# Attention's gating on VectorE in two steps, and the sample tile's LayerNorm on VectorE

## The chip, the cores and the metric

The kernel runs on one core of a Trainium2 chip. Its time is the device time of one execution in microseconds (us); the figure that counts is the median of several executions. Six units work side by side and meet at semaphores: TensorE (PE, with PEld for its weight loads), VectorE (DVE), ScalarE (ACT), GpSimd (POOL), SyncE (SP, which here only issues transfers) and the DMA engines. Each engine takes its own instructions strictly in their order. SP, ACT and POOL each issue transfers from that same order, so an issue that has to wait also holds what stands behind it.

## The reference

A two-layer decoder step for a prompt of 2048 rows and 8 samples of 8 rows (64 rows), model width 1024. Layer 0 ("even") has a pooling mixer and a differential attention with 4 heads; layer 1 ("odd") is a gated linear attention. What the change touches is the end of the attention's head and the layer's LayerNorm:

```python
o = diff_attn_prompt(qf, kf, vf, lam_full)        # softmax(q1 k1) - lambda softmax(q2 k2), times v
o = (rms_norm(o, subln_w) * (1.0 - lam_init)).reshape(b, t, DA_WIDTH).astype(x.dtype)
mix = jnp.concatenate([pool_out * jax.nn.silu(pg), o * jax.nn.silu(ag)], axis=-1)
y = layer_norm(DN_ALPHA * x + mix @ w_out, ln_g, ln_b)
```

So each row of a head's output (128 values) is scaled by one over its root mean square and multiplied by a gate, silu(ag), value by value. The LayerNorm then works on rows of 1024.

## The kernel before

The even layer runs in four stretches. First the input projection, to about 540 us, with head 0's first work woven in. Then head 0 of the attention beside out_pool, the pooling half of the output projection (to about 740). Then head 1 beside Sample, the samples' own attention over cached keys and values (to about 890). Then heads 2 and 3 beside out_attention, which is the attention half of the output projection and the LayerNorm (to about 1236). The odd layer fills the rest.

`weave` (L861) interleaves a main generator (Attention.units, L1109) with a fill generator by declared costs. The program so built is then put in order by a scheduler that simulates it, with the scores of the attention given priority. So a change of which engine does a step changes the order on every engine, wherever the simulated times move.

In `Attention`, the 16 tiles t of 128 query rows are taken one after the other, each for the heads of the stretch. `load_q` (L971) loads 256 rows of queries by two transfers on SP's queue into qr (two buffers), which `split` (L37) cuts into a high part qh on ScalarE and a low part ql on GpSimd; `load_gate` (L985) loads the gate of the same 256 rows, sga (four buffers), on SP's queue. `scores` (L992) makes the scores sc on PE (L1016, L1017), their row maximum nm on VectorE and the exponentials e on ScalarE (L1036). `pv` (L1056) transposes e on PE (tp, L1068), copies the result on ScalarE (aT) and multiplies it by the values (po, L1061). It then copies po to oq (L1088) and sums its squares on VectorE (sqq, L1090). After each second tile, `rms_scale` (L2309) makes the row scale rmo from both tiles' sums: small VectorE steps L2320, L2322, a power on GpSimd (L2333) and VectorE L2325. Then come the gating steps that are changed, on oq of 128 x 2 x 128. For heads 0 and 1 a GpSimd transfer writes oq to memory; heads 2 and 3 leave it in place for out_attention. There are 16 tiles and 4 heads, so 32 such pairs.

In `out_attention`, `tile_` (L1221) transposes one row tile of the mixed heads on PE (otp, L1227: two from om, loaded from memory, and two from oq of heads 2 and 3), splits it into oh and ol, multiplies it by the output weights (op, L51 to L53) and calls LayerNorm's `finish` (L1284). The row tiles come in the order 0 to 13, 16, 14, 15, where tile 16 is the 64 sample rows. `turn` (L1237) transposes the finished rows for the odd layer. `finish` has two ways to apply root, mean, gain and bias to z: four VectorE steps in two halves with one transfer each on SP's and ScalarE's queues (urgent, L1293 to L1301), or three GpSimd steps over all 1024 values and a GpSimd transfer (L1302 to L1305).

`Sample` (L2098) loads its inputs on SP's queue: the page table, the samples' queries and new keys (sqr, skn), the new values (svn), constants, and then for every page the cached keys (sk) and values (sv), to addresses that SP reads from the page table. Its first products on PE are ssc (L2170), from sk.

## Time and profile before

| | before |
|---|---|
| median of 3 runs | 2129.9 us (2129.59 to 2132.04) |
| profiled execution | 2135.73 us |
| its span, first to last instruction | 2133.9 us |
| mean granted TensorE clock | 0.975 of full speed |
| TENSOR_SCALAR L1097 (gating, GpSimd) | 64 instructions, median 367 ns |
| TENSOR_TENSOR L1099 (gating, GpSimd) | 32 instructions, median 734 ns |

The profile is that of one execution. A row of the timeline gives the start, the duration, the engine, the line, the operation and its tiles (out<-in), the count of instructions that the row groups, and in square brackets how long the engine stood idle before it and what released it. In a row of waits stand who waited for whom, the sum, the number of waits and the longest. A row of a group gives its sum and the mean of one in ns; a row with three numbers divided by strokes gives minimum, median and maximum in ns. Rows of queues end in "q": SPq is SyncE's own list of transfers, and the duration there is that of the issue. The groups quoted with 14 or 64 instructions are those between 560 and 1232 us.

### The profile page before, as it was taken

What the parts mean: (1) busy time and instruction counts of PE and PEld (TensorE: products, weight loads), DVE (VectorE), ACT (ScalarE), POOL (GpSimd) and SP (SyncE); (2) the same over time, 40 slices, a digit from 0 to 9 for tenths busy, and PEclk for the clock granted to TensorE, in tenths of its full rate; (3) what the DMA queues carried; (4) which work ended last, traced back from release to release, by engine and by line L of the source; (5) the groups of instructions that cost most, each with busy time, mean ns of one, the idle gap of its engine ahead of it and who ended that gap; (6) DMA issues with size and microseconds to landing.
All of it is one profiled execution on the core that took longest, in us unless ns stands there. A gap on an engine that the chain in (4) does not pass through costs nothing. (4 is left out here: it accounts for less than half of the span.)

```text
span 2133.9 us, 31445 instructions
## 1 busy us (share of the span) xinstructions
PE 2005.8 (94%) x10769; PEld 1641.6 (77%) x10769; DVE 1486.8 (70%) x2762; ACT 1005.2 (47%) x1910; POOL 878.9 (41%) x1163
## 2 busy tenths in 40 slices
PE   8999998999999999888898899999999997999998
PEld 7878786877788777677777678788888776888786
DVE  7697657565876676798767667756733647888884
ACT  4244433345633465665555443445425655555552
POOL 2345444323754542567643504222211223466554
PEclk9999999999899999999999999999999998999998
DMA  8877777547864588563322458765643557556532
GB/s 288 278 241 238 256 260 233 168 110 198 276 203 152 169 294 284 157 202 121 119 72 65 146 187 281 253 205 199 198 146 121 180 163 242 165 170 204 164 130 109
DMA packets 210973, 407.75 MB, mean 191 GB/s; under 512 B 29186, under 2 KB 106370, under 8 KB 210802
## 3 DMA queue, kind: packets, MB, share of 16 engines
q1 hardware_dynamic: 140354, 234.57, 36.1%
q0 software_dynamic: 49664, 156.39, 20.8%
q10 hardware_dynamic: 20784, 14.68, 2.2%
q8 instruction: 87, 1.43, 0.3%
q14 instruction: 84, 0.69, 0.1%
HBM read 277.99 MB, written 127.55 MB: 190 GB/s over the span
## 5 line engine op out<-in xcount | busy, mean ns | idle before, releaser
L1036 ACT ACTIVATE e<-sc,nm 128x896 f32<-128x896 f32 (+11 forms) x192 | 164.8, 864 | 125.5 <-DVE nm L1034 87.3
L1021 DVE TENSOR_REDUCE nm<-sc 128x1 f32<-128x768 f32 (+7 forms) x160 | 156.8, 991 | 27.9 <-PE sc L1017 16.3
L45 DVE TENSOR_TENSOR wk<-wr,wk 128x1024 fp32r<-128x1024 f32 x80 | 98.3, 1229 | 101.3 <-ACT wk L40 100.8
L45 DVE TENSOR_TENSOR wl<-wr,wh 128x1024 fp32r<-128x1024 f32 (+1 forms) x90 | 108.7, 1211 | 80.7 <-ACT wh L40 76.8
L1016 PE MATMUL sc<-kst,qh 128*128 128x512 f32 (+9 forms) x352 | 136.5, 391 | 29.3 <-ACT e L1036 28.2
L1061 PE MATMUL po<-vt,aT 128*128 128x128 f32 x1088 | 155.4, 282 | 2.2 <-ACT aT L1073 2.1
L40 ACT ACTIVATE wh<-wr 128x1024 fp32r<-128x1024 f32 (+1 forms) x85 | 88.0, 1038 | 138.7 <-PE f L52 62.4
L1061 PEld LDWEIGHTS po<-vt,aT 128*128 128x128 f32 x1088 | 140.4, 197 | 9.0 <-ACT aT L1073 2.4
L40 ACT ACTIVATE wk<-wr 128x1024 fp32r<-128x1024 f32 x77 | 81.4, 1058 | 134.1 <-PE f L53 96.2
L1073 ACT ACTIVATE aT<-tp 128x512 f32<-128x512 f32 (+3 forms) x160 | 85.4, 534 | 103.0 <-PE tp L1068 102.4
L1017 PE MATMUL sc<-kst,ql 128*128 128x512 f32 (+9 forms) x352 | 123.8, 354 | 0.0
L1016 PEld LDWEIGHTS sc<-kst,qh 128*128 128x128 f32 x352 | 69.3, 197 | 49.9 <-ACT e L1036 40.6
L1068 PE MATMUL tp<-ident,e 128*128 128x128 f32 x544 | 92.4, 285 | 13.1 <-ACT aT L1073 11.8
L1045 DVE SCALAR_TENSOR_TENSOR e<-e,c,e 128x128 f32<-128x128 f32 (+15 forms) x64 | 96.0, 1499 | 1.4
L1068 PEld LDWEIGHTS tp<-ident,e 128*128 128x128 f32 x544 | 64.5, 145 | 28.2 <-ACT aT L1073 16.7
L1017 PEld LDWEIGHTS sc<-kst,ql 128*128 128x128 f32 x352 | 69.7, 198 | 4.1 <-issue 0.2
L1039 DVE TENSOR_TENSOR s<-s 128x1 f32<-128x1 f32 x64 | 21.2, 331 | 70.2 <-ACT e L1036 69.9
L1092 POOL TENSOR_SCALAR s1q<-s 128x1 f32<-128x1 f32 x64 | 16.9, 266 | 104.4 <-DVE s L1039 79.5
L53 PE MATMUL op<-wh,ol 128*128 128x512 f32 x128 | 52.3, 408 | 5.1 <-DVE ol L1232 5.1
L51 PE MATMUL op<-wh,oh 128*128 128x512 f32 x128 | 53.1, 415 | 1.2 <-ACT oh L1231 1.2
L51 PE MATMUL gz<-wh,gmh 128*128 128x512 f32 x128 | 51.5, 406 | 1.8 <-ACT gmh L40 1.8
L53 PE MATMUL gz<-wh,gml 128*128 128x512 f32 x128 | 51.1, 402 | 1.9 <-DVE gml L45 1.9
(882 smaller groups left out, 6658.2 us busy)
## 6 DMA issues: line engine op xcount, KB each, us to landing
wr<-in_w_q SPq DMA_DIRECT2D x75, 512.0 KB, 4.9
wr<-pt SPq DMA_DIRECT2D x40, 512.0 KB, 7.3
wr<-rt SPq DMA_DIRECT2D x40, 512.0 KB, 4.2
sk<-in_cachek SPq DMA_DIRECT2D x64, 256.0 KB, 3.7
sv<-in_cachev SPq DMA_DIRECT2D x64, 256.0 KB, 4.8
pt<-pn POOLq DMA_DIRECT2D x32, 256.0 KB, 7.2
qr<-q SPq DMA_DIRECT2D x64, 128.0 KB, 3.9
kr<-k SPq DMA_DIRECT2D x32, 256.0 KB, 4.4
```

The costliest lines, as they stand in the source:

```text
L40: h = nc.scalar.activation(hi, raw, AF.Copy)
L45: return h, (lo_eng or nc.vector).tensor_tensor(out=lo, in0=raw, in1=hi, op=ALU.subtract)
L51: nc.tensor.matmul(ps, lh(k), rh(k), start=(first and k == 0), stop=False, **kw)
L53: nc.tensor.matmul(ps, ll(k), rh(k), start=False, stop=(last and k == n - 1), **kw)
L1016: nc.tensor.matmul(o, qh[:, c, qs], kst[:, ks], start=True, stop=False)
L1017: nc.tensor.matmul(o, ql[:, c, qs], kst[:, ks], start=False, stop=k < npc - 1)
L1021: nc.vector.tensor_reduce(out=nm[:, c, i:i + 1], in_=p[:, :, :w], op=ALU.max, axis=AX.XY, negate=True)
L1036: nc.scalar.activation(o, p, AF.Exp, bias=nm[:, m, 0:1], accum_out=s[:, m, i if npc > 1 else 0:][:, :1])
L1045: nc.vector.scalar_tensor_tensor(out=es[0][:, :nk], in0=es[1][:, :nk], scalar=c2, in1=es[0][:, :nk], op0=ALU.mult, op1=ALU.add)
L1061: nc.tensor.matmul(po, s[:, 128 * j:128 * j + 128], vt[:, k0 + j, :], start=(k0 + j == 0), stop=(k0 + j == n - 1))
L1068: nc.tensor.transpose(p[:, 128 * j:128 * j + 128], a[:, 128 * (k0 + j):128 * (k0 + j) + 128], self.ident)
L1073: nc.scalar.activation(s[:, :128 * g], p[:, :128 * g], AF.Copy)
```

## The change

Two edits. In `pv`, two GpSimd steps that scale each of the two tiles by its rows' factor, and one GpSimd step that multiplies both by the gate, become two VectorE steps, one per tile, that do both at once. In `tile_`, the list of tiles that take LayerNorm's urgent way is widened from 14 and 15 to all above 13, which adds tile 16.

```diff
@@ Attention.pv
             for i in range(2):
-                nc.gpsimd.tensor_scalar(out=oq[:, i, :], in0=oq[:, i, :], scalar1=sc[:, i:i + 1], scalar2=1.0,
-                                        op0=ALU.mult, op1=ALU.mult)
-            nc.gpsimd.tensor_tensor(out=oq, in0=oq, in1=sg, op=ALU.mult)
+                nc.vector.scalar_tensor_tensor(out=oq[:, i, :], in0=oq[:, i, :], scalar=sc[:, i:i + 1], in1=sg[:, i, :],
+                                               op0=ALU.mult, op1=ALU.mult)
@@ out_attention.tile_
-        ln.finish(d["y0"][t0:t0 + n, :], i in (14, 15))
+        ln.finish(d["y0"][t0:t0 + n, :], i > 13)
```

From line 1098 on, every line of the new program has a number lower by one (L1097 is the new gating step, L1227 becomes L1226, L2325 becomes L2324, and so on). The scheduler's order changes with it; two places show this.

The first is SP's queue early in head 1, at the loads ahead of the sample's cache keys. In the names, qr_5, qr_6 and qr_7 are head 1's query loads for its last three blocks of 256 rows (two transfers each, in two buffers), sga_2 is the gate of its third block, kr are keys, zr and zx belong to out_pool, and pages and sqr to Sample. Before:

```order
L977 DMA qr_5_7714<-q_57 64x2x256 x2
L1171 DMA zx_0_6447<-in_x 64x512
L963 DMA kr_1_9574<-k_58 64x2x512 x2
L1171 DMA zx_1_6448<-in_x 64x512
L977 DMA qr_6_8075<-q_57 64x2x256 x2
L2106 DMA pages<-in_page_table 1x64
L2112 DMA sqr<-q_57 64x4x64
```

And with the change:

```order
L1170 DMA zx_0_6440<-in_x 64x512
L963 DMA kr_1_9557<-k_58 64x2x512 x2
L977 DMA qr_6_8063<-q_57 64x2x256
L1170 DMA zx_1_6441<-in_x 64x512
L977 DMA qr_6_8063<-q_57 64x2x256
L977 DMA qr_7_8447<-q_57 64x2x256 x2
L989 DMA sga_2_7013<-sg_60 128x2x128
L2105 DMA pages<-in_page_table 1x64
L2111 DMA sqr<-q_57 64x4x64
```

Two loads of qr_7 and one of a gate, sga_2, now stand between qr_6 and the page table; before, they stood behind the first cache loads.

The second is VectorE at the end of the attention, where oq_2 and oq_3 are the last tiles of heads 2 and 3 and oz is the sample tile's row block. Before:

```order
L1278 SCALAR_TENSOR_TENSOR oz_12535,lnso_16_12863<-oz_12535,op_1_12875 64x512
L1090 SCALAR_TENSOR_TENSOR sqq_2_12657,ssq_2_12367<-oq_2_12366 128x128
L1288 TENSOR_SCALAR lnso_16_12863<-lnso_16_12863 64x1
L2320 TENSOR_TENSOR rmoa_2_12660<-rmoa_2_12660,ssq_2_12367 128x2
L2322 TENSOR_SCALAR rmoa_2_12660<-rmoa_2_12660 128x2
L2325 TENSOR_TENSOR rmoa_2_12660<-rmoa_2_12660,rmra_2_12661 128x2
L1291 TENSOR_SCALAR lnso_16_12863<-lnso_16_12863 64x1
L1090 SCALAR_TENSOR_TENSOR sqq_3_12719,ssq_3_12459<-oq_3_12458 128x128
```

And with the change:

```order
L1287 TENSOR_SCALAR lnso_16_12831<-lnso_16_12831 64x1
L1290 TENSOR_SCALAR lnso_16_12831<-lnso_16_12831 64x1
L1295 SCALAR_TENSOR_TENSOR oz_12505<-oz_12505,lnso_16_12831,lng 64x512 x2
L1090 SCALAR_TENSOR_TENSOR sqq_2_12627,ssq_2_12337<-oq_2_12336 128x128
L1297 SCALAR_TENSOR_TENSOR oz_12505<-oz_12505,lnso_16_12831,lnb 64x512 x2
L2319 TENSOR_TENSOR rmoa_2_12630<-rmoa_2_12630,ssq_2_12337 128x2
L2321 TENSOR_SCALAR rmoa_2_12630<-rmoa_2_12630 128x2
L2324 TENSOR_TENSOR rmoa_2_12630<-rmoa_2_12630,rmra_2_12631 128x2
L1097 SCALAR_TENSOR_TENSOR oq_2_12336<-oq_2_12336,rmoa_2_12630,sga_7_11730 128x128 x2
L1090 SCALAR_TENSOR_TENSOR sqq_3_12688,ssq_3_12429<-oq_3_12428 128x128
```

The four LayerNorm steps of the sample and the gating of head 2's last tiles now stand on VectorE ahead of sqq_3. On PE, the transposes of oq_2 and oq_3 for row tile 14 (otp) stood one behind the first eight products po of head 3's last tile and one behind all of them:

```order
L1061 MATMUL po_3_12673<-vt_8755,aT_3_4_12686 128x128 x4
L1227 MATMUL otp_12916<-ident,oq_2_12366 128x128
L1068 MATMUL tp_3_12_12703<-ident,e_3_0_12375 128x128 x4
L1061 MATMUL po_3_12673<-vt_8755,aT_3_8_12697 128x128 x4
L1061 MATMUL po_3_12673<-vt_8755,aT_3_12_12708 128x128 x4
L1227 MATMUL otp_12916<-ident,oq_3_12458 128x128
```

And with the change both stand behind them:

```order
L1068 MATMUL tp_3_12_12672<-ident,e_3_0_12345 128x128 x4
L1061 MATMUL po_3_12642<-vt_8741,aT_3_8_12666 128x128 x4
L1061 MATMUL po_3_12642<-vt_8741,aT_3_12_12677 128x128 x4
L1226 MATMUL otp_12886<-ident,oq_2_12336 128x128
L1226 MATMUL otp_12886<-ident,oq_3_12428 128x128
```

Only the place of the first transpose has moved there.

## The prediction

> **What bounds the kernel now.** I read the busy shares first, then the windows by stage, then TensorE's waits in the stages that the diff touches, and last the timeline around the longest of them.
>
> ```profile
> PE 2005.8 (94%) x10769; PEld 1641.6 (77%) x10769; DVE 1486.8 (70%) x2762; ACT 1005.2 (47%) x1910; POOL 878.9 (41%) x1163
> 560.00:740.00 180.00, 176.91 (x1000) 149.67 (x998) 125.32 (x246) 74.74 (x164) 95.71 (x137) 0.98 0.64 194
> 740.00:880.00 140.00, 132.30 (x1419) 99.85 (x1418) 96.32 (x275) 81.19 (x202) 48.04 (x81) 0.99 0.82 260
> 920.00:1200.00 280.00, 251.68 (x1552) 212.71 (x1552) 219.57 (x460) 153.65 (x328) 149.44 (x156) 0.98 0.34 106
> 1200.00:1240.00 40.00, 30.13 (x164) 25.05 (x164) 25.02 (x46) 19.79 (x36) 18.86 (x18) 0.83 0.65 202
> 1240.00:1300.00 60.00, 60.00 (x277) 49.46 (x276) 39.99 (x71) 19.59 (x33) 10.68 (x18) 1.00 0.57 190
> ```
>
> The columns after a window's length are the busy time of PE, PEld, DVE, ACT and POOL, then the granted clock, the DMA share and GB/s. PE is the bound: 94% of the whole. The changed steps run from 560 to 1230 us. In head 0 (560 to 740) PE is idle for 3.1 us, in head 1 (740 to 880) for 7.7, in heads 2 and 3 (920 to 1200) for 28.3 us, with VectorE next at 219.57 of 280 and GpSimd at 149.44. From 1200 to 1240 PE is idle a quarter of the time, at a clock of 0.83; from 1240 on it is busy without a break. So what PE gains or loses up to 1240 stands in the end time, and GpSimd's 41% by itself is worth nothing: what counts is the waits of PE that end on it.
>
> ```profile
> PE sc L1016 <- ACT e L1036: 10.8, 10, 2.9
> PE otp L1227 <- POOL oq L1099: 7.8, 3, 6.1
> ```
>
> These are PE's two largest waits from 920 to 1232. The first is the softmax chain, which the change doesn't touch in itself. The second ends on the very GpSimd step that the change removes, 7.8 us in three waits, of which one is 6.1. That one is the tail of attention:
>
> ```profile
> 1216.04 0.54 POOL L2333 TENSOR_TENSOR lnso<-lnso,rsqeo 64x1 f32<-64x1 f32 x1
> 1218.72 2.01 PE L1061 MATMUL po<-vt,aT 128*128 128x128 f32 x16
> 1220.76 0.28 ACT L1088 ACTIVATE oq<-po 128x128 f32<-128x128 f32 x1 [1.25 <-PE po L1061]
> 1220.95 2.33 POOL L1304 TENSOR_TENSOR oz<-oz,lnb 64x1024 f32<-64x1024 f32 x1
> 1221.07 2.36 DVE L1090 SCALAR_TENSOR_TENSOR sqq<-oq 128x128 f32<-128x128 f32 x1 [5.12 <-ACT oq L1088]
> 1223.92 0.71 POOL L2333 TENSOR_TENSOR rmoa<-rmoa,rsqea 128x2 f32<-128x2 f32 x1 [0.64 <-DVE rmoa L2322]
> 1225.25 0.71 POOL L1097 TENSOR_SCALAR oq<-oq,rmoa 128x128 f32<-128x128 f32 x2
> 1226.83 0.48 PE L1227 MATMUL otp<-ident,oq 128*128 128x128 f32 x1 [6.10 <-POOL oq L1099]
> 1223.40:1233.60 10.20, 6.09 (x14) 4.59 (x15) 4.92 (x13) 5.49 (x10) 2.72 (x5) 0.50 0.74 242
> ```
>
> PE ends its last product at 1220.73 and stands until 1226.83. In between: the copy of oq, its square sum sqq on VectorE, which here lasts 2.36 us beside the sample LayerNorm's L1304, the power on GpSimd, and the three gating steps. After such a stand the clock is halved: 0.50 for the 10.2 us of the last row.
>
> **The change part by part.**
>
> ```profile
> L2250 DVE SCALAR_TENSOR_TENSOR ssq<-so,rmos,ssg x8: 339/341/1353, 900.5 to 903.6; 128x128 f32<-128x128 f32 x8
> L1090 DVE SCALAR_TENSOR_TENSOR sqq<-oq x64: 264/286/2496, 562.3 to 1221.1; 128x128 f32<-128x128 f32 x64
> L1090 DVE SCALAR_TENSOR_TENSOR sqq<-oq 128x128 f32<-128x128 f32 x64 | 33.5, 523 | 9.2 <-ACT oq L1088 8.9
> 1212.54 0.68 DVE L1278 SCALAR_TENSOR_TENSOR oz<-oz,op 64x512 f32<-64x512 f32 x1
> L1303 POOL TENSOR_TENSOR oz<-oz,lng 128x1024 f32<-128x1024 f32 x14 | 34.3, 2447 | 0.8
> L1304 POOL TENSOR_TENSOR oz<-oz,lnb 128x1024 f32<-128x1024 f32 x14 | 35.5, 2538 | 0.5
> L1097 POOL TENSOR_SCALAR oq<-oq,rmoa 128x128 f32<-128x128 f32 x64 | 27.2, 433 | 13.1 <-DVE rsqea L2332 6.1 <-DVE rmoa L2325 2.8 <-DVE c L1043 1.6
> L1099 POOL TENSOR_TENSOR oq<-oq,sga 128x256 f32<-128x256 f32 x32 | 26.9, 844 | 1.3
> ```
>
> The new gating step has the form of L2250 (two SBUF tensors, a scalar per row, 128x128): 0.341 us. VectorE gets 64 x 0.341 = 21.8 us, and 4 x 0.68 = 2.7 us for the sample's LayerNorm. GpSimd loses 27.2 + 26.9 = 54.1 us of gating, and the sample's steps.
>
> **1. The tail, a gain.** Worked forward from these rows. The sample's root is there at 1216.58. VectorE's four new LayerNorm steps and the square sum of the third head, which the order puts among them, take 4 x 0.68 + 0.29 = 3.0, to 1219.6. The third head's scale and gating follow: 0.45 for two small steps, 0.74 with the power, 0.26 for the last factor, 0.68 for two gating steps, to 1221.7. PE doesn't wait for this, since its transpose now stands behind the last products. The fourth head's oq is there at 1221.04, so VectorE is 0.7 late; its square sum ends at 1222.1, the power starts at 1222.55 and ends at 1223.3, the gating ends at 1224.15, and PE starts at 1224.25 in place of 1226.83: **-2.6 us**. The gap falls from 6.1 to 3.5 us. The halved stretch is 10.2 us, of which 6.8 follow the restart and cost 3.4 us of work; I take **-1.0** for it, between 0 and -3.4, because the restart now falls earlier into a stretch that may still begin. From 1240 on no other engine holds PE, so the gain carries.
>
> [...]
>
> **2. Head 1's last query load, a gain.** The order moves two loads of qr_7 on SP's queue from amid the cache loads to ahead of the page table.
>
> ```profile
> 817.41 0.63 ACT L40 ACTIVATE qh<-qr 128x512 fp32r<-128x512 f32 x1 [6.30 <-DMA qr<-q]
> 818.98 0.46 PE L1016 MATMUL sc<-kst,qh 128*128 128x416 f32 x1 [2.55 <-ACT e L1036]
> 820.60:824.00 3.40, 3.40 (x16) 1.47 (x15) 3.36 (x5) 0.89 (x3) 0.56 (x1) 0.51 0.92 301
> ```
>
> ScalarE stood 6.30 us before this split, with the exponentials queued behind it, and PE 2.55 us for those; a window at 0.51 followed and cost 1.7 us of its 3.4. With the load some 80 us earlier both go: **-4.3 us**, at least 0 if another wait takes that place.
>
> **3. The price of that move.** SP takes its loads in order. In the new order qr_7 (two loads) and then sga_2 wait for a buffer, and the page table, the sample's inputs and the cache keys stand behind them.
>
> ```profile
> 714.92 1.23 SPq L977 DMA_DIRECT2D qr<-q  x2
> 716.20 0.49 SPq L2106 DMA_DIRECT2D pages<-in_page_table  x1
> 718.71 0.68 SPq L2112 DMA_DIRECT2D skn<-k  x1
> 725.18 0.47 SPq L2121 DMA_DIRECT2D svn<-v  x1
> 726.96 0.38 SPq L2131 DMA_DIRECT2D smask<-in_s_mask  x1
> 728.46 16.93 SPq L2142 DMA_DIRECT2D sk<-in_cachek  x10
> 729.69 1.26 POOL L45 TENSOR_TENSOR ql<-qr,qh 128x512 fp32r<-128x512 f32 x1
> 729.75 1.23 DVE L2325 TENSOR_TENSOR rmoa<-rmoa,rmra 128x2 f32<-128x2 f32 x1
> 731.88 0.34 SPq L2142 DMA_DIRECT2D sk<-in_cachek  x1
> DMA to landing us min/median/max: 3.0/3.2/3.4
> 742.75 1.06 PE L2170 MATMUL ssc<-sk,sqs 128*32 128x512 f32 x8
> ```
>
> Two query buffers exist, so qr_7 waits for head 1's ql two loads earlier, done at 730.95. sga_2 waits for the gating of head 0's rows right behind L2325, which with two VectorE steps is done at 731.7. Page table, sample inputs and the small constants then take what they took before (716.20 to 719.4 and 725.18 to 727.3: 5.4 us, and a further 1.1 to the first key load at 728.46; the wait between them is for PE and is over by then), so the first key load comes at about 739.2 and the fourth, 731.88 before, at 742.6, landed at 745.8 with 3.2. PE asks at 742.75: a stand of 3.1, in place of a slack of 7.7. Part of a later wait for the softmax is absorbed, part comes back as a halved window of 1.7: **+4.0**, between 0 (if the buffers come free sooner) and +8 (each us beyond that point is one of PE's).
>
> **4. The transpose wait in head 3.**
>
> ```profile
> 1112.84 0.33 PE L1227 MATMUL otp<-ident,oq 128*128 128x128 f32 x1 [1.50 <-POOL oq L1099]
> ```
>
> Its 1.50 us go, but for the new steps' own length: **-1.3**.
>
> **5. VectorE's new work.** Half of the 21.8 us, 10.9, fall where VectorE is busy 219.57 of 280. Below heads 0 and 1 PE is busy at least 94% of its time, and that hides the other half. How much of 10.9 reaches PE no row shows: at least 0, since 60 us of VectorE are idle there and the steps leave GpSimd, which shortens its queue for everyone; at most 10.9 and the holds. L1090 shows the holds: 286 ns by the median, 523 by the mean, 2496 at most, beside GpSimd steps. L1303 and L1304 take 69.8 us of the 280, a quarter; of 16 pairs of new steps 4 would meet one, at half its 2.5 us: 5 us. So 0 to +16; I take **+2.5**, the quarter of 10.9 by which VectorE's idle share is not enough, since a step can only delay PE if the softmax chain is then late. GpSimd's removed steps held VectorE too, which goes the other way and is in the lower end.
>
> [...]
>
> **6.** The order also changes inside the odd layer (the first 60 us and around 1800), without new work: 0, within 3 either way.
>
> Sum: -2.6 - 1.0 - 4.3 + 4.0 - 1.3 + 2.5 = **-2.7 us**. The profiled execution took 2135.73 (span 2133.9 and 1.8 around it), 5.8 over the median of the runs; it would become 2133.0, and the median 2129.9 becomes **2127.2**.
>
> **The rivals.**
> - **More is gained:** the key loads are not late (term 3 is 0: no stand at the first ssc), the halved windows at the tail go (-3.4) and VectorE's idle time takes the new steps (term 5 is 0): -2.7 - 4.0 - 2.4 - 2.5 = -11.6, 2118.3. For it speaks that each wait named is a measured one; against it, that VectorE's idle time in heads 2 and 3 is in pieces around a chain which PE already waits on, 10.8 us.
> - **The queue eats it:** SP stands longer than I think (term 3 at +8): +1.3, 2131.2. It decides when the first keys land past 750.
> - **Slower: VectorE becomes the wait in heads 2 and 3.** The new steps sit ahead of the row maxima that the exponentials need. If all 10.9 us and the holds of 5 land on PE, term 5 is +16: -2.7 + 13.5 = +10.8, 2140.7; with half of that +4, 2133.9. It passes the -2.7 of the rest as soon as over 5.2 of those 16 us reach PE, and shows slower from about 9.5. The softmax wait of 10.8 us with VectorE at 78% speaks for it; that the removed GpSimd steps held VectorE too speaks against it.
> - **It doesn't do what it says:** PE waits for the transposes elsewhere as much as before, with the tail alone at -1: terms 1 and 4 nearly nothing, +1, 2131. Little speaks for it, since the wait's releaser is removed.
>
> **How the numbers follow.** About 0.2%, 4.3 us, can be told from no change: 2125.6 to 2134.2. The forecast has 0.42, with an own range of 2122 to 2132 (a third of it below 2125.6); more is gained 0.24; the queue eats it 0.07; slower 0.23; not as said 0.04. Faster: 0.24 + 0.14 = 0.38. Slower: 0.22, with 0.01 of that rival inside the bound. The same: the rest, 0.40. The range reaches half way into both outer cases, 2116 to 2138.
>
> **What would show it.** Tail: the wait of otp on oq at 3.5 us, released by VectorE L1097, sqq at 0.29, no GpSimd step of 2.3 us beside it. Head 1: no ScalarE wait for qr near 817. SP: qr_7 about 731, the first key load about 739, a PE wait for sk of about 3 us. Heads 2 and 3: VectorE's sum up by some 11 us, PE's wait for e at 10.8 to 14. I am wrong if that wait grows by over 8, if the keys come later than 745, or if new steps of 2 us and more stand in a row.

## The result, and the profile after

| | before | after |
|---|---|---|
| median of 5 runs each | 2129.59 us (2128.41 to 2132.04) | 2153.94 us (2152.93 to 2160.76) |
| ratio of after to before | | 1.0117, 95% interval 1.0104 to 1.013 |
| profiled execution | 2135.73 us | 2160.76 us |
| its span | 2133.9 us | 2159.0 us |
| mean granted TensorE clock | 0.975 | 0.969 |

The changed kernel is slower by 24.4 us, where 2.7 us less had been forecast. One run of a later kernel, that with heads 0 and 1 changed, took 2290.72 us at a granted clock of 0.825 and counts in no median or ratio here. The profiled execution of the changed kernel is 6.8 us over its median, that of before 6.1, so the two profiles can be compared. First the busy shares of the changed kernel, as the page gives them:

```profile
PE 2019.4 (94%) x10769; PEld 1650.6 (76%) x10769; DVE 1501.9 (70%) x2830; ACT 1006.6 (47%) x1910; POOL 811.1 (38%) x1063
```

By these GpSimd lost 68 us of work (878.9 before) and VectorE took 15 (1486.8). TensorE has the same 10769 matmuls, but they last 14 us longer, and its mean granted clock is lower (0.969 against 0.975). So I looked for the stage in which that happens. These are the windows of the changed kernel, with the columns as in the prediction (the third after the colon is PE's busy time, the last three numbers are granted clock, DMA share and GB/s):

```profile
560.00:740.00 180.00, 175.84 (x991) 148.62 (x992) 123.59 (x264) 74.39 (x164) 83.33 (x119) 0.98 0.62 188
740.00:880.00 140.00, 133.57 (x1437) 100.61 (x1435) 101.42 (x287) 82.53 (x207) 37.18 (x61) 1.00 0.85 274
880.00:930.00 50.00, 36.76 (x197) 29.32 (x195) 42.06 (x107) 27.80 (x75) 28.95 (x30) 0.73 0.74 217
930.00:1200.00 270.00, 236.23 (x1425) 200.06 (x1424) 208.09 (x431) 137.91 (x295) 110.41 (x101) 0.95 0.28 86
```

And those windows of the kernel before which the prediction hasn't shown:

```profile
880.00:930.00 50.00, 37.25 (x244) 30.96 (x237) 44.54 (x107) 32.21 (x85) 36.38 (x42) 0.90 0.70 217
930.00:1200.00 270.00, 243.75 (x1496) 205.88 (x1496) 211.01 (x431) 146.66 (x311) 141.84 (x147) 0.98 0.31 97
```

Up to 880 us hardly anything is lost. From 880 to 930 the clock is 0.73 in place of 0.90, and 197 matmuls start in place of 244; from 930 to 1200 it is 0.95 in place of 0.98, and 1425 start in place of 1496. VectorE's share of the second window is no larger (208.09 of 270 us against 211.01), though it is a share of less work.

Windows of equal length hold unequal work, so I cut both traces after equal numbers of matmuls instead, at the start of the 4520th and of the 6640th (the end of head 1 to just behind the attention). These are nearly the same matmuls: ahead of the first cut 16 of the 4520 differ, ahead of the second 2 of the 6640. The same view, first of before, then of after:

```profile
0.00:865.82 865.82, 825.19 (x4520) 664.97 (x4523) 600.11 (x1133) 378.53 (x702) 372.39 (x615) 0.98 0.73 228
865.82:1252.16 386.34, 337.47 (x2130) 282.76 (x2121) 295.40 (x609) 209.50 (x452) 202.57 (x211) 0.96 0.40 125
1252.16:2133.90 881.74, 843.13 (x4131) 693.85 (x4129) 591.33 (x1020) 417.19 (x757) 303.98 (x338) 0.97 0.55 184
```
```profile
0.00:867.30 867.30, 826.19 (x4520) 665.07 (x4521) 604.05 (x1165) 379.42 (x704) 345.81 (x573) 0.99 0.72 228
867.30:1272.64 405.34, 347.48 (x2130) 289.60 (x2121) 311.50 (x646) 209.46 (x449) 164.79 (x152) 0.92 0.38 119
1272.64:2159.00 886.36, 845.75 (x4131) 695.94 (x4129) 586.30 (x1020) 417.76 (x757) 300.48 (x338) 0.97 0.54 183
```

Of the 25.1 us between the spans, 19.0 lie in the middle stretch (405.34 against 386.34), 1.5 ahead of it and 4.6 behind. The 1.3 us by which after is late at the 2000th matmul (489.6 against 488.3), ahead of the first changed step, are in the 1.5. In the middle the matmuls are busy 10.0 us longer (347.48 against 337.47), and PE's idle time, length less busy, goes from 48.9 to 57.9 us. So about half of the loss is more waiting, and half is the clock, which is halved for 65 us of the stretch in place of 34. VectorE works 16.1 us more there (311.50 against 295.40), 77% and 76% of the stretch. PE's waits from 880 to 1262 of after, then of before without its largest wait for oq, which the prediction shows:

```profile
PE sc L1016 <- ACT e L1036: 18.3, 21, 3.0
PE op L53 <- DVE ol L1231: 11.4, 5, 3.7
PE tp L1068 <- ACT aT L1073: 11.2, 16, 1.8
PE po L1061 <- ACT aT L1073: 5.0, 3, 4.0
PE otp L1226 <- DVE oq L1097: 4.2, 2, 2.4
PE tp L1068 <- DVE e L1045: 3.2, 1, 3.2
```
```profile
PE sc L1016 <- ACT e L1036: 18.1, 16, 3.4
PE tp L1068 <- ACT aT L1073: 8.0, 14, 0.8
PE op L53 <- DVE ol L1232: 5.1, 5, 2.1
PE po L1061 <- ACT aT L1073: 2.1, 2, 1.8
```

The wait for the gating fell from 7.8 to 4.2 us, as meant. The wait for the softmax's exponentials is the same. What grew are waits for steps that the change doesn't touch: the low parts ol for out_attention (+6.3), the transposed exponentials aT (+3.2 and +2.9), one wait for e (3.2, new). None of them is large; they are spread over the stretch.

The largest single one stands where head 1 ends. The timeline of after around it:

```profile
894.44 4.50 DVE L2249 SCALAR_TENSOR_TENSOR ssq<-so,rmos,ssg 128x128 f32<-128x128 f32 x3
896.26 5.08 POOL L969 TENSOR_TENSOR kst<-kr,kst 64x512 fp32r<-64x512 f32 x4
898.87 0.94 DVE L1024 TENSOR_REDUCE nm<-sc 128x2 f32<-128x768 f32 x1
899.92 0.58 ACT L1036 ACTIVATE e<-sc,nm 128x384 f32<-128x384 f32 x1 [1.21 <-DVE nm L1024]
901.13 1.67 PE L1061 MATMUL po<-vt,aT 128*128 128x128 f32 x8 [3.95 <-ACT aT L1073]
```

and its windows right behind:

```profile
901.60:928.90 27.30, 21.61 (x80) 16.11 (x79) 20.84 (x67) 13.29 (x37) 8.81 (x12) 0.50 0.92 288
```

Three of the eight gating steps of the *samples* (L2249, unchanged by the diff) stand ahead of a row maximum nm on VectorE. They take 4.50 us beside GpSimd's kst, 1.5 each in place of 0.34; the maximum, the exponential and the transposed copy are late, and PE stands 3.95 us. Then the clock is halved (0.50) for 27.3 us. Before, the order had that maximum ahead of all eight steps, at 899.64, and they then took 3.42 us together. ScalarE's wait for the keys kr just before, 1.53 us, is in this trace too.

### The profile page after: what moved, and what is told of

Read it like the earlier page. It is cut to its first block, busy times and chain, and to the rows that moved or that the text cites. A ratio compares the mean times of both kernels' runs of the same rounds, so it can differ in the third digit from the quotient of the medians.

```text
span 2159.0 us, 31437 instructions
## 1 busy us (share of the span) xinstructions
PE 2019.4 (94%) x10769; PEld 1650.6 (76%) x10769; DVE 1501.9 (70%) x2830; ACT 1006.6 (47%) x1910; POOL 811.1 (38%) x1063
## 5 line engine op out<-in xcount | busy, mean ns | idle before, releaser
L1039 DVE TENSOR_TENSOR s<-s 128x1 f32<-128x1 f32 x64 | 23.8, 371 | 49.0 <-ACT e L1036 48.9
L45 POOL TENSOR_TENSOR ql<-qr,qh 128x512 fp32r<-128x512 f32 x31 | 40.3, 1303 | 45.0 <-ACT qh L40 38.7
L2332 POOL TENSOR_TENSOR rmoa<-rmoa,rsqea 128x2 f32<-128x2 f32 x32 | 24.1, 752 | 78.1 <-DVE rmoa L2321 70.1
```

What stands on the lines that cost most here:

```text
L45: return h, (lo_eng or nc.vector).tensor_tensor(out=lo, in0=raw, in1=hi, op=ALU.subtract)
```

## The experiments

Ratios are to the kernel before, run on the same chip, with 95% intervals.

### Which part loses: each edit alone

The prediction's third rival says that VectorE's new steps hold up heads 2 and 3 from where they stand. The first four kernels take the change apart. One has the gating edit without the LayerNorm edit:

```diff
# after, without the second edit
-        ln.finish(d["y0"][t0:t0 + n, :], i > 13)
+        ln.finish(d["y0"][t0:t0 + n, :], i in (14, 15))
```

> The changed kernel without its second edit: gating by two VectorE steps, the sample tile's LayerNorm by GpSimd as before. The full change measured 2153.9 against 2129.6, and its trace puts nearly all of the 24 us between 890 and 1240 us. Theory 1 (VectorE's new steps in heads 2 and 3 are the loss): 2150 to 2160, the tail's gain gone. Theory 2 (a new order of the work, in which something unlucky happens near 900 us and the clock is halved for 27 us): near 2150 if the order there is the same as in the full change, else anything from 2125 to 2155. Theory 3 (the sample's LayerNorm is the loss): about 2130.

One has the LayerNorm edit alone:

```diff
# before, with the second edit
-        ln.finish(d["y0"][t0:t0 + n, :], i in (14, 15))
+        ln.finish(d["y0"][t0:t0 + n, :], i > 13)
```

> The kernel before with the second edit alone: the sample tile's LayerNorm by VectorE. Theories 1 and 2: 2124 to 2130, the gain at the tail of some 3 us or nothing. Theory 3: 2145 or more.

And two have the new gating for two heads only, heads 0 and 1 (which run ahead of the stretch that loses) or heads 2 and 3 (which run in it):

```diff
# before, with the new gating for some heads: h < 2 in the one, h >= 2 in the other
+            if h < 2:
+                for i in range(2):
+                    nc.vector.scalar_tensor_tensor(out=oq[:, i, :], in0=oq[:, i, :], scalar=sc[:, i:i + 1], in1=sg[:, i, :],
+                                                   op0=ALU.mult, op1=ALU.mult)
+            else:
...
```

> The kernel before with the new gating for heads 0 and 1 alone; in heads 2 and 3 the work is the same as before, on the same engines. Theory 1 (VectorE's new steps in heads 2 and 3): within 4 us of 2130, since PE hides heads 0 and 1. Theory 2 (order): heads 2 and 3 have a new order although their work is that of before, so 2140 or more.

> The kernel before with the new gating for heads 2 and 3 alone; SP's loads early in head 1 stand as before. Theory 1 (VectorE's new steps in heads 2 and 3): 2145 to 2155. Theory 2 (order): the arrangement near 900 us is that of before, the clock keeps its full rate there, and the time is 2120 to 2135.

| kernel | median us | ratio |
|---|---|---|
| gating alone, all heads | 2154.72 | 1.0122 (1.0084 to 1.016) |
| LayerNorm edit alone | 2133.20 | 0.9997 (0.9979 to 1.0014) |
| gating of heads 0 and 1 | 2152.35 | 1.0099 (1.0062 to 1.0136) |
| gating of heads 2 and 3 | 2131.82 | 1.0002 (0.9986 to 1.0019) |

The third rival falls. With all the new steps of heads 2 and 3 on VectorE in the very stretch that it named, the time doesn't move by more than the interval. The loss comes with heads 0 and 1. Yet it isn't lost *in* them. The window between the same two cuts, of the kernel with heads 0 and 1 changed:

```profile
863.25:1263.52 400.27, 344.67 (x2130) 288.52 (x2121) 291.82 (x610) 209.33 (x449) 198.72 (x204) 0.92 0.38 120
```

Head 1 ends at 863.25 us, 2.6 earlier than before, and then 13.9 us are lost in heads 2 and 3, whose own gating still is on GpSimd there. What can reach from heads 0 and 1 into that stretch is the order: in that trace PE, VectorE and ScalarE take the stretch's instructions in another order than before, though the work there is that of before. That the scheduler's simulated times have moved is the likely reason; no run shows that simulation. That became the theory; its rivals were single places in that order.

A further kernel joins the two parts that cost nothing, in case their gains add up:

```diff
# before, with the second edit and the new gating for h >= 2
+            if h >= 2:
...
+        ln.finish(d["y0"][t0:t0 + n, :], i > 13)
```

> The parts of the change that cost nothing, together: new gating for heads 2 and 3, and the sample tile's LayerNorm on VectorE. The order near 895 us is that of before (all eight sample steps behind the row maximum). Predicted for the tail: the wait of 6.1 us at 1220 us falls to 3.5. By that: 2126 to 2131. If the tail's gain is lost in the spread of the clock: 2130 to 2135.

It took 2135.47 us, 1.0012 (0.9995 to 1.0029): level with before. Its trace shows why the tail's gain is not there to see: the last wait for oq falls to 2.90 us, but 18 us earlier PE waits 5.77 us for a transposed copy aT.

### Is it one head, and is it VectorE at all?

New gating for head 1 alone, and for head 0 alone:

```diff
# before, with the new gating for one head: h == 1 in the one, h < 1 in the other
+            if h == 1:
+                for i in range(2):
+                    nc.vector.scalar_tensor_tensor(out=oq[:, i, :], in0=oq[:, i, :], scalar=sc[:, i:i + 1], in1=sg[:, i, :],
+                                                   op0=ALU.mult, op1=ALU.mult)
+            else:
...
```

> The kernel before with the new gating for head 1 alone. SP's loads early in head 1 stand as before, but the order in heads 2 and 3 is again with tile 0 of the out-projection ahead, near to that of e3_gate01. Theory O: 2138 to 2155, as e3_gate01. If it is the moved query load and cache keys (SP's order in head 1) that decide: 2128 to 2135.

> The kernel before with the new gating for head 0 alone. SP's loads early in head 1 stand as in the changed kernel (the query load ahead of the page table), the order in heads 2 and 3 is a third one. If the loss goes with that order of SP's loads, or if the parts add up (e8_head1 lost 7 of the 22 of e3_gate01): 2143 to 2150. If each order in heads 2 and 3 has a loss of its own by its waits and windows (theory K): anything from 2130 to 2155, and then in step with the mean granted clock: with a clock of 0.977 near 2132, with 0.970 near 2148.

Head 1 alone: 2140.02 us, 1.0042 (1.0027 to 1.0057). Head 0 alone: 2136.32 us, 1.0013 (0.9999 to 1.0027). Together they had 1.0099, more than both added.

The traces of these kernels say something about order by themselves. Between the two cuts, the kernel with head 1 changed has nearly the order of that with heads 0 and 1 (99 of 100 instructions of PE, VectorE and ScalarE stand in the same sequence by their tiles and shapes). Its stretch is long as well, 396.07 us, though no gating of head 0 has moved:

```profile
860.95:1257.02 396.07, 337.06 (x2131) 281.61 (x2121) 293.41 (x610) 209.25 (x449) 199.08 (x204) 0.94 0.39 121
```

And PE's waits are nearly the same, kind by kind: from 866 to 1262 us it waits 28.8 and 27.5 us for e, 7.4 and 7.4 for aT ahead of the transposes, 5.5 and 5.6 ahead of the products. What differs is the halved time, 44 us and 65, and the time ahead of the stretch and behind it. Head 0 alone has an order of its own, and 382.85 us. The other pairs of one order agree too: before and the LayerNorm edit alone have 386.34 and 388.03 us, after and the gating alone 405.34 and 404.57, heads 2 and 3 without and with the LayerNorm edit 387.99 and 385.32.

The other way round: nothing goes to VectorE, but GpSimd's gating of heads 0 and 1 is cut into four steps in place of three:

```diff
# before, for h < 2
             for i in range(2):
                 nc.gpsimd.tensor_scalar(out=oq[:, i, :], in0=oq[:, i, :], scalar1=sc[:, i:i + 1], scalar2=1.0,
                                        op0=ALU.mult, op1=ALU.mult)
-            nc.gpsimd.tensor_tensor(out=oq, in0=oq, in1=sg, op=ALU.mult)
+                nc.gpsimd.tensor_tensor(out=oq[:, i, :], in0=oq[:, i, :], in1=sg[:, i, :], op=ALU.mult)
```

> The kernel before, with the gating of heads 0 and 1 still on GpSimd but in four steps in place of three (scale and gate for each of the two tiles): no new work for VectorE, some 0.3 us more for GpSimd at each of 16 pairs. Its order in heads 2 and 3 is nearer to that of the changed kernel than to that of before: tile 0 of the out-projection ahead of tile 2 of head 2. Theory O (order): 2138 to 2155. Theory E (VectorE's steps in heads 0 and 1): 2128 to 2136.

2137.41 us, 1.0032 (1.0005 to 1.006). One more step per pair on an engine that is busy 41% of its time makes the kernel a little slower as well. That is consistent with a new order as the cause, though it doesn't exclude a price of the steps themselves.

### Which place in the order: out_attention's transposes

In the changed program the first transposes otp of all row tiles but the last stand elsewhere among the products po of heads 2 and 3 than before. Two kernels test it from both sides, at nine row tiles. In the first the work is changed (the gating alone), and each of the nine transposes is to be tied behind a product near which it stands in the order before; in the second the work is that of before, and products are tied so that transposes come half a row tile ahead:

```diff
# the gating edit alone, with transposes tied to where before has them
+AFTER = {0: (2, 2), 1: (3, 4), 2: (2, 5), 3: (2, 6), 4: (2, 7), 5: (3, 7), 13: (3, 14), 16: (2, 15), 14: (3, 15)}
...
+                with tc.issue_after(A.po_first.get(at, A.po_last).ins):
+                    nc.tensor.transpose(tp[:, 128 * k:128 * k + n], src, ident[:n, :n])
```

> e1_gating (2154.7 against 2132.3) with the out-projection's tiles held back on PE: the first transpose of nine row tiles is tied behind the product po behind which it stood in the kernel before (tile 0 behind tile 2 of head 2, and so on; two of them one product earlier than before). The work and its engines are those of e1_gating. Theory O (the loss comes from the order in heads 2 and 3, the out-projection standing half a row tile or more ahead of the heads it should cover): the loss from about 930 us on goes, some 10 to 14 us, and the time is 2136 to 2145, with what is left due to the event near 893 us (a wait of PE of 4 us and the halved clock after it). Theory E (the order on PE doesn't matter, VectorE's steps in heads 0 and 1 do, by what they delay): 2150 to 2158.

```diff
# before, with the first product of nine (head, tile) pairs tied behind a row tile's transpose
+BEHIND = {(2, 2): 0, (2, 4): 1, (2, 5): 2, (2, 6): 3, (3, 6): 4, (3, 7): 5, (3, 14): 13, (2, 15): 16, (3, 15): 14}
...
+                with self.tc.issue_after(at.ins) if at else ExitStack():
+                    nc.tensor.matmul(po, s[:, 128 * j:128 * j + 128], vt[:, k0 + j, :],
+                                     start=(k0 + j == 0), stop=(k0 + j == n - 1))
```

> The kernel before, its work and engines untouched, with the products of heads 2 and 3 held back on PE behind the out-projection's transposes, at nine places taken from e1_gating's order (tile 0 keeps its place, the others move half a row tile ahead, and from tile 7 on the order is neither's). Theory O: slower than before, 2136 to 2150. Theory E, or if only the event near 893 us counts: 2128 to 2135.

The first took 2161.05 us, 1.0127 (1.0105 to 1.0149): no better than after. But its tie only did part of what was meant. Counted by the po matmuls ahead of them in the trace, the transposes of tiles 0, 13, 16 and 14 stand where before has them; those of tiles 1 to 3 stand where after has them, and 4 and 5 (656 and 672 of these matmuls) between after (642 and 664) and before (664 and 688). So this run says nothing about tiles 1 to 5. The second took 2136.13 us, 1.0023 (1.0006 to 1.004), a fifth of the loss; in its trace tiles 1 to 5 stand 12 to 16 po matmuls ahead of before, close to after, and 13, 16 and 14 have not moved.

Two other traces are a better test. The kernel with head 0 changed (1.0013) and the first of those tied by order further down (1.0108) have the transposes of tiles 0 to 4 at the same places (behind 556, 584, 612, 628 and 650 po matmuls). Where these stand doesn't decide the loss.

### Which place: the samples' gating and the wait near 898 us

Next the event that the timeline shows. Take the samples' eight steps off VectorE, so that no row maximum can stand behind them: to ScalarE (eight scalings, then one multiply on GpSimd), or all to GpSimd:

```diff
# after
         for n in range(8):
-            nc.vector.scalar_tensor_tensor(out=sq[:, n, :], in0=self.o[:, n, :], scalar=sc[:, n:n + 1], in1=sg[:, n, :],
-                                           op0=ALU.mult, op1=ALU.mult)
+            nc.scalar.activation(sq[:, n, :], self.o[:, n, :], AF.Copy, scale=sc[:, n:n + 1])
+        nc.gpsimd.tensor_tensor(out=sq, in0=sq, in1=sg, op=ALU.mult)
```

> The changed kernel with the sample's own gating (eight VectorE steps at the end of head 1's stretch) made by eight steps of ScalarE and one of GpSimd. In the changed kernel three of those steps, held beside GpSimd's key split, stand ahead of a row maximum near 895 us; PE then waits 3.95 us and its clock is halved for 27.3 us. The ten traces so far show when: a clock window of 3.41 us in which PE is busy under about 0.47 is followed by a halved one, and the clock comes back only after a halved window in which PE is busy over about 0.82. Theory K (short waits of PE in heads 2 and 3, made long by that clock, are most of the loss): this wait goes, the halved stretch is 10 us or less, and the time is 2135 to 2147. Theory R (the rest of the new order in heads 2 and 3 loses the time by waits spread over it): 2150 to 2158.

```diff
# after, all of it on GpSimd
+            nc.gpsimd.tensor_scalar(out=sq[:, n, :], in0=self.o[:, n, :], scalar1=sc[:, n:n + 1], scalar2=1.0,
+                                    op0=ALU.mult, op1=ALU.mult)
+        nc.gpsimd.tensor_tensor(out=sq, in0=sq, in1=sg, op=ALU.mult)
```

> The changed kernel with the sample's own gating made by GpSimd (eight steps and one) in place of VectorE: a second way of taking those steps out of VectorE's queue, with another order in heads 2 and 3 than e9_ssqact. If the one place is the cause: 2130 to 2140, as e9_ssqact (2134.2). If e9_ssqact was only a lucky order: anything up to 2155; GpSimd's steps delay the key split by some 5 us, which can cost 2 to 4.

And the counter-test: before, with the one order edge that makes the event, so that the maximum of tile 2 of head 2 stands behind three of the eight steps (SSQ holds the third of them):

```diff
# before
+                        with self.tc.issue_after(SSQ[-1].ins) if (t, h) == (2, 2) else ExitStack():
+                            nc.vector.tensor_reduce(out=nm[:, :, 0], in_=p[:, :, :w], op=ALU.max, axis=AX.X, negate=True)
```

> The kernel before, its work and engines untouched, with one edge of order on VectorE: the row maximum of tile 2 of head 2 stands behind three of the sample's eight gating steps, as in the changed kernel, where before it stood ahead of all eight. If that one place is the cause: a wait of PE of 3 to 4 us near 895 us with a halved clock of 10 us or more behind it, and 2140 to 2152. If it only goes with the rest of the new order: 2130 to 2136.

| kernel | median us | ratio |
|---|---|---|
| after, samples' gating on ScalarE | 2134.17 | 1.0000 (0.9982 to 1.0018) |
| after, samples' gating on GpSimd | 2138.75 | 1.0025 (1.0011 to 1.0039) |
| before, with the event | 2135.94 | 1.0010 (0.9997 to 1.0024) |

The first alone would have made a good story: the event is gone, and so is the loss. The other two speak against it. On GpSimd the loss shrinks to a fifth although a long halved stretch is still there at the same place. The window of that kernel:

```profile
901.20:925.10 23.90, 19.12 (x64) 13.30 (x65) 18.25 (x47) 12.68 (x34) 10.23 (x15) 0.50 0.67 222
```

And before with the event forced on it loses nothing that can be told from no change. Its wait there is 2.6 us, shorter than the 3.95, and the clock is halved for 6.8 us behind it in place of 27.3, so it isn't a full copy of the event. That place of the three steps alone, at least, doesn't make the loss.

### Does the clock make the loss? Idle products on TensorE

If half of the loss is the clock, work that keeps PE busy should buy some of it back. Two idle products (128x384, written to an unused part of po's bank) stand ahead of the last products of tiles 0 to 5 of heads 2 and 3, 24 in all. They were put into after, and for comparison into the kernel with only heads 2 and 3 changed:

```diff
# after in the one; before with the new gating for h >= 2 in the other
...
+        if h >= 2 and t < 6:
+            for _ in range(2):
+                nc.tensor.matmul(spare, self.qs[h, t // 2][0][:, 0, :128], self.kst[h][0][:, :384],
+                                 start=n <= 4, stop=n <= 4, skip_group_check=n > 4)
         products(*pend)
```

> The changed kernel with 24 idle products more on PE (two of 128x384 ahead of the last products of each of tiles 0 to 5 of heads 2 and 3, written to a part of po's bank that nobody reads; some 0.33 us each, 8 us in all), put where PE waits for ScalarE's copies. Theory K: PE's windows there get fuller, the halved time from 888 to 930 falls from 27 to under 12 us and the time falls although work was added, to 2140 to 2150. Theory R: 2155 to 2165, the added work on top.

> e4_gate23 (new gating for heads 2 and 3 alone, 2131.8 against 2132.3) with the same 24 idle products. Theory K: the halved time early in heads 2 and 3 (10 us there) falls to some 3 us, worth 2 to 4 us, against up to 8 us of added work of which the waits hide half: 2128 to 2136. Theory R: 2135 to 2141.

Windows of the first:

```profile
880.00:930.00 50.00, 38.69 (x306) 31.77 (x305) 41.06 (x109) 30.80 (x82) 30.93 (x31) 0.90 0.71 208
930.00:1200.00 270.00, 237.37 (x1437) 201.61 (x1436) 203.59 (x445) 142.18 (x301) 116.24 (x105) 0.96 0.30 91
```

2149.43 us, 1.0065 (1.0041 to 1.009), against 1.0117 for after: the clock from 880 to 930 is back at the 0.90 of before (after: 0.73), and the loss is down by about half, from 1.17% to 0.65%. In the other kernel, which hadn't lost, they change nothing: 2133.33 us, 0.9995 (0.9979 to 1.0011). That fits a clock that makes about half of the loss. It doesn't show it: the added products also changed the order, and orders alone differ by as much, as the next kernels show.

### The same instructions in another order

The last three kernels settle whether it is order at all. They are the changed kernel with no instruction added, removed or moved to another engine (in the traces PE has 10769, VectorE 2830, ScalarE 1910 and GpSimd 1063, as in after). The samples' eight steps are tied on VectorE behind the row maximum of one (tile, head): (2, 2), (2, 3) or (3, 2). SSQ lists the eight steps, x is the maximum; the edge sets the order and asks for no semaphore.

```diff
# after; (2, 2), (2, 3) or (3, 2)
...
+                        if (t, h) == (2, 2):
+                            for y in SSQ[0:]:
+                                self.tc.add_manual_dep(y.ins, x.ins.name,
+                                                       mybir.DependencyInfo(mybir.DependencyClass.NoSync,
+                                                                            mybir.DependencyReason.DATA),
+                                                       reason="order")
```

> The changed kernel, its work and engines untouched, with the sample's eight gating steps tied on VectorE behind the row maximum of tile 2 of head 2, as they stood before. If the loss is one of order and that place decides: the wait of 3.95 us of PE near 897 us and the 27 us of halved clock go, 2132 to 2145. If the work that moved to VectorE costs the time: 2150 to 2158.

> The same with the eight steps behind the row maximum of tile 2 of head 3, 4 to 6 us later. Loss by order: 2130 to 2145, and not the same as e16_behind22, since the rest of the order in heads 2 and 3 differs. Loss by work: 2150 to 2158.

> The same with the eight steps behind the row maximum of tile 3 of head 2. Loss by order: 2130 to 2145. Loss by work: 2150 to 2158.

| tied behind the maximum of | median us | ratio |
|---|---|---|
| tile 2, head 2 | 2158.48 | 1.0108 (1.0079 to 1.0137) |
| tile 2, head 3 | 2138.03 | 1.0015 (0.9998 to 1.0033) |
| tile 3, head 2 | 2141.96 | 1.0040 (1.0022 to 1.0057) |

The same work on the same engines takes anything between 1.0015 and 1.0108 of before, and 1.0117 in after. The windows between the same two cuts, of (2, 2) first, then of (2, 3):

```profile
867.85:1269.43 401.58, 344.63 (x2130) 288.58 (x2120) 301.88 (x646) 209.36 (x449) 166.09 (x152) 0.92 0.39 120
```
```profile
869.31:1256.13 386.82, 338.47 (x2130) 283.31 (x2121) 293.76 (x646) 209.59 (x449) 169.92 (x152) 0.94 0.39 124
```

With the second order the stretch takes 386.82 us, that of before (386.34), with all of the change's steps on VectorE. The same 646 VectorE instructions are busy 293.76 us there, 301.88 in (2, 2) and 311.50 in after, so how long they take depends on the order too. That isn't the loss by itself: heads 0 and 1 alone lost with 291.82. Both have the same wait near 898: PE's po waits 2.6 us for aT in either, behind a ScalarE step that waits 1.5 us for the keys kr, and the clock is then halved for 20.5 us. One loses 1.1% and the other 0.15%, so that wait doesn't decide either. From 880 to 930 (2, 2) also waits 8.9 us for e, (2, 3) 3.5. PE's waits from 930 to 1262, of (2, 2), then of (2, 3):

```profile
PE sc L1019 <- ACT e L1045: 13.2, 11, 3.2
PE tp L1077 <- ACT aT L1082: 8.4, 10, 1.5
PE tp L1077 <- DVE e L1054: 4.7, 3, 1.8
PE op L53 <- DVE ol L1240: 4.1, 3, 2.8
```
```profile
PE sc L1019 <- ACT e L1045: 9.9, 9, 2.7
PE tp L1077 <- ACT aT L1082: 8.5, 11, 1.6
PE op L53 <- DVE ol L1240: 8.4, 7, 2.5
PE tp L1077 <- DVE e L1054: 1.0, 1, 1.0
```

Here the fast order waits longer for ol than the slow one (8.4 against 4.1), the opposite of before and after. No single kind of wait goes with the loss through all of these kernels.

What does go with it is the time at half clock between the two cuts. In the five traces whose stretch takes 400 us or more (after, gating alone, heads 0 and 1, the first kernel with tied transposes, and (2, 2)) it is 55 to 65 us; in the thirteen others without idle products, with stretches of 383 to 396 us, it is 27 to 48. PE's idle time overlaps more: 56 to 66 us in the five, 48 to 59 in the others. This is a correlation over one execution of each. It doesn't say which of the two comes first.

## Why the prediction was wrong

The named steps came out as follows, by the profile of after.

- **1, the tail: right, and more than forecast.** PE's last wait for oq is 2.35 us (forecast 3.5, before 6.10), released by L1097. The timeline of after around it:

```profile
1246.23 0.29 DVE L1090 SCALAR_TENSOR_TENSOR sqq<-oq 128x128 f32<-128x128 f32 x1 [2.95 <-ACT oq L1088]
1247.01 0.70 POOL L2332 TENSOR_TENSOR rmoa<-rmoa,rsqea 128x2 f32<-128x2 f32 x1 [4.58 <-DVE rmoa L2321]
1247.93 0.61 DVE L1097 SCALAR_TENSOR_TENSOR oq<-oq,rmoa,sga 128x128 f32<-128x128 f32 x2
1248.34 0.33 PE L1226 MATMUL otp<-ident,oq 128*128 128x128 f32 x1 [2.35 <-DVE oq L1097]
```

  VectorE had nothing queued ahead of sqq, which starts 0.03 us behind its input's end; the forecast had it 0.7 us late. The halved stretch behind the wait is one window of 3.4 us in place of 10.2. Still, the LayerNorm edit by itself, with that wait at 3.72, gives 0.9997 (0.9979 to 1.0014): 2 us are less than that interval tells.
- **2, head 1's last query load: right in its wait, its gain is not shown.** No ScalarE wait for qr is left near 817, nor the halved window behind it. PE's idle time from 740 to 880 falls from 7.7 to 6.4 us, with the next term in it. But from the 3200th to the 4520th matmul before takes 136.3 us and after 136.4, so by the end of head 1 nothing of 4.3 us is to be seen (16 of those matmuls differ).
- **3, the price on SP's queue: right in place, too large.** The loads of SP in the timeline of after, and PE's wait from 740 to 880:

```profile
716.63 14.74 SPq L977 DMA_DIRECT2D qr<-q  x3
731.48 0.57 SPq L989 DMA_DIRECT2D sga<-sg  x1
738.54 7.53 SPq L2141 DMA_DIRECT2D sk<-in_cachek  x7
```
```profile
PE ssc L2169 <- DMA sk<-in_cachek: 1.7, 1, 1.7
```

  The first key load comes at 738.54 (forecast 739.2; with the gate's own 0.57 the forecast's steps add up to 738.8), and PE stands 1.7 us where 3.1 were forecast, with no halved window behind it (clock 1.00 from 740 to 880). So the stand is +1.7, not +4.0.
- **4, the transpose wait in head 3: gone as forecast**, in the 4.2 us that are left of 7.8.
- **5, VectorE's new work: +2.5 lies within what the runs allow, its rival doesn't.** One new step takes 0.345 us by the median (forecast 0.341), with single ones up to 2.58:

```profile
L1097 DVE SCALAR_TENSOR_TENSOR oq<-oq,rmoa,sga x64: 331/345/2580, 577.4 to 1248.2; 128x128 f32<-128x128 f32 x64
```

  All 64 take 27.4 us, against 21.8 worked out. Two of them take 2.47 and 2.58 us, beside the LayerNorm steps L1302 and L1303 on GpSimd. But gating of heads 2 and 3 alone, in an order of its own, costs 1.0002 (0.9986 to 1.0019), at most 4 us. Holds are there, and no more of them than that reaches PE's end time. Single VectorE steps beside the removed GpSimd steps had been long as well: before, one L1039 (128x1) at 1096.57 takes 0.73 us beside L1099's 0.74, where the median of the 64 is 0.16.
- **6, the order: this step failed.** It was written for the odd layer only, "0, within 3 either way", and heads 2 and 3 were taken to keep the order of before but for the places quoted. In fact the order of that whole stretch is drawn anew. By the profiles that is worth +13.9 us in the stretch with heads 0 and 1 changed alone, and +19.0 with all of the change, as two terms which the sum didn't have: 9.0 us of more waits and 10.0 of a lower clock. The clock had been priced at the tail, with 1.0 us, and behind the two waits of terms 2 and 3, with 1.7 each; in heads 2 and 3 ahead of the tail it had no price. The odd layer itself, for which the term was written, is 4.6 us longer in the one profile of each; over the eighteen traces without idle products it takes 878 to 888 us, so 4.6 tells little.

So the sum's named waits were good to within a few us. The bounds were too narrow because the order of heads 2 and 3 was left out. The prediction's own signs of being wrong didn't show it either: the wait for e went from 18.1 to 18.3 us, the keys came at 738.54, and the long new steps don't stand in a row. The rival that forecast "slower" had the right sign and the right stage, and a mechanism that the runs don't bear out.

What is shown: the loss comes with the gating of heads 0 and 1, arises for the most part (19.0 of 25.1 us between the profiles) in heads 2 and 3, and goes to a level that can't be told from before by order alone (1.0015) with every instruction kept. What stays open: which place of the new order makes it. Neither the first transposes of out_attention, as far as they were tested, nor the samples' steps near 895, nor the wait at 898 decides by itself, and the waits that grow differ from kernel to kernel. That many short waits are made costly by the clock is argued from the windows, the halved times and the idle products, not from one run that isolates it. No kernel tried is faster than before; the best are level with it.

## What to carry to other kernels

Where a scheduler sets the order from simulated times, a change in one stage can be a new draw of the order in the stages behind it. Here four orders of the same instructions took 1.0015 to 1.0117 of the time before. The spread of 1%, some 20 us, is more than all the waits that the change was worked out from. Give such a change a term of its own in the forecast, sized by the stages behind it in which the busiest engine already waits, and compare both traces after equal numbers of matmuls before explaining any single wait. If an edit loses in a stage that it doesn't touch, try the same instructions under one or two other orders before giving the edit up.

## What the hardware showed

What follows is counted from the granted clock of TensorE in the traces of this case. In all 20 of them the halved stretches lie on a grid of 3.41 us, the same through one execution and shifted from one execution to the next; but for the one that ends the trace, they are 3.41 to 13.65 us long before (17 of them) and 3.41 to 27.31 after (19). For each grid window I took PE's busy share from its matmul records, and the clock of the next one. A full-rate window with PE busy under 0.40 was followed by a halved one 219 of 219 times, one of 0.40 to 0.45 40 of 43 times, 0.45 to 0.50 45 of 80, 0.50 to 0.60 23 of 190, and above 0.60 16 of some 11300, 15 of them in the last 20 us of a trace. A halved window with PE busy under 0.82 was followed by another halved one 208 of 209 times, and one of 0.90 or more once in 302 (the halved stretch that ends a trace is left out). By these counts I estimate that a wait of about 2 us that fell well into one window (0.60 of 3.41 us is 2.0) was enough here for a halved one to follow. A halved stretch could last long with PE mostly busy: in the 27.3 us after 901.60 PE was busy 21.61 us, 79%, at half rate. From 880 to 1260 before and after have about as many full-rate windows under 0.45 (6 and 7), but 10 halved ones before and 19 after: in 2 of the halved windows before and 9 after PE was busy under 0.82, and another halved one followed each.

The same program scatters, and its time goes with the clock: the runs of the kernel before in this study lie between 2124.62 and 2143.17 us, and those under 2130 us had a granted clock of 0.979 in the mean, those over 2135 one of 0.976. A profile shows one execution, so a difference of 5 us between two spans says nothing by itself.
